# One decoder step on one core: rotary step, softmax scaling, norm squares and residual sums taken from GpSimd, scores of the sample grouped, last squares through TensorE

## The chip, the cores and the metric

One Trainium2 chip, one core of it. The metric is the device time of one execution in microseconds (us), as the median of several runs. TensorE is called PE here, VectorE DVE, ScalarE ACT, GpSimd POOL; SP is the queue from which most transfers are issued.

## The reference, cut to what matters

One layer of a decoder over 264 tokens (256 of a prompt, 8 of a sample, one each), width 2048, all in float32:

```
h = rms_norm(x, g1);  z = h @ w_in          # q (8 heads x 128), k/v of three branches (2 KV heads), gates, u
q, k = partial_rope(first 32 of 128 dims)
o  = sum over 3 branches of gate * softmax(q k / sqrt(128)) v   # compressed blocks, selected blocks, window
d  = pooled mixer of u
m  = concat(o, d) @ w_o
x  = x + rms_norm(m, g2)
a  = relu(rms_norm(x, g3) @ w_up) ** 2      # 2048 -> 8192
y  = x + rms_norm(a @ w_down, g4)           # 8192 -> 2048
```

With 256 prompt tokens all selected blocks are chosen, so the selected branch is plain causal attention. The sample's 8 tokens attend to 256 cached rows each, of both branches, read through a page table. The new cache rows and the window state are outputs too.

## The kernel before, in words

**Linear layers.** Activations lie transposed, features on the 128 partitions and the 264 tokens in the free dimension. Each float32 weight chunk (1 MB, 512 x 512) arrives in a `raw` tile and is converted half by half: ACT writes the rounded high part `wh` (line 195), DVE the rest `wl` (line 193). `linear()` (line 213 on) forms four output tiles in four PSUM banks (`pm`) by three products (high x high, high x low, low x high), each 128 x 264: 24 matmuls per half of a chunk, in four steps of six. All are on line 236. I call the 24 matmuls of one half "a half". The half's two conversions are issued about two halves ahead (`conv_to`).

**What sets the order.** The order is written out by hand. `run()` goes through the steps of a linear layer; at each it calls `tick()`, which does what `later()` put off (evacuations, squares, gains), and then advances the side streams (generators such as `scores00`, `rope_q00`, `sample`, `norm2`) whose entries in the table `AT` (line 36) are due at that step number. Steps 232 to 263 are the last input projection z_q1, 264 to 327 the pool half of w_o, 328 to 391 its attention half, 392 to 423 the first quarter of w_up. Each engine works through its own list in order.

**Attention.** `rope()` (line 500 to 503) rotates 32 partitions of two heads: a shuffle, two products, a sum; of the four calls for q, two are wholly on DVE, and two leave the second and the fourth operation (lines 501 and 503) to POOL. `scores(g, i)` (g: KV head, i: block of 128 queries; a "unit") puts q k into a `px` bank (line 805, two banks in all), adds the mask on DVE, takes the exponential on ACT (line 791), and multiplies each of three parts (16 compressed keys, the selected keys, the window's keys) by the reciprocal sum times the gate `den` (line 824): two parts on DVE, the window's on POOL. `values()` transposes the parts by PE (line 848), evacuates them as high and low halves (`th`, `tl`) and multiplies by the values (lines 208 to 210); the 16 compressed keys go in plain float32 (line 841). `sample_attn()` transposes the cached keys of each of 8 samples and of two branches (line 943), copies them to `kt_` (two buffers), and multiplies each branch's by the two KV heads' queries (`score()`, line 932): 16 calls of two matmuls.

**Norm between w_o and w_up.** The last quarter of w_o is added into `mT` (DVE), each tile squared on ACT, the squares added to `acc0` on POOL (`accumulate()`, line 1162). The last tile's square and the two before are added on DVE (`last_squares`, lines 1175 to 1177) and both sums go through PE, in three banks of one column (line 1221). `rstd_of()` makes 1/sqrt by ACT and DVE. Three DVE operations put it on a diagonal `dg` (line 1239); PE times a matrix of ones spreads it over the partitions (line 1245, tile `pr2`). For each of 16 feature tiles `h2_x` forms mT * r on DVE (line 1258) and adds it to the residual `xT` on POOL (line 1260; the first two on DVE); `h2_hi` rounds on ACT (line 1263), `h2_lo` takes the rest on DVE (line 1268). `h2_before` calls these two tiles at a time, once per half of the first quarter of w_up. Meanwhile halves of the first w_up chunks are converted into spare tiles `xc`, one low part on POOL (`pool_lows`).

**Second norm.** At steps 424 to 443 the stream `norm2` squares the 16 tiles of `xT` on ACT and adds them on POOL (line 1162); its sums go through PE at line 1198.

**Tail.** The last quarter of w_down is added to `m2` (line 1404) and multiplied by the gain (line 1407); the last squares go as above, through three banks (line 1425). Of the eight output pieces of 128 x 512, six are y + o * r on DVE (line 1458), two are a product on ACT and a sum on POOL (line 1452); the sample's outputs (`ts`, `tt`) are made on POOL and transposed by PE (line 1438).

## Time and profile before

| what | value |
|---|---|
| median of 3 runs | 1178.67 us (1178.59 to 1181.34) |
| the profiled execution | 1180.37 us |
| its span in the trace | 1178.6 us |
| mean granted clock of PE | 0.992 |
| PE busy | 1150.8 us, 98% |
| share of PE line 236 in the chain of waits | 71% |
| DVE, ACT, POOL busy | 58%, 46%, 11% |

The profile gives each engine's busy time, the waits of each engine with the instruction that released it, the chain of work that ended last, and for any stretch the busy times with the clock that PE was granted. A share over the whole span says little here: PE has work for nearly all of it, so time can only go where PE waits, where it runs at the lower clock, or where an instruction on PE is dearer than it has to be. These places are few and lie between 205 and 452 us and at the end.

### The profile page before, as it was taken

To read this page: it belongs to the slowest core of one execution; us is meant where nothing else is said; L and a number is where in the kernel's file an instruction comes from. 1 tells how busy PE (TensorE), PEld (TensorE's weight loads), DVE (VectorE), ACT (ScalarE), POOL (GpSimd) and SP (SyncE) were. 2 spreads that over 40 slices of the span, in tenths; PEclk is the share of its full clock that TensorE was granted. 3 is DMA by queue.
4 is the path that set the end of the run, shared out by engine and by line. 5 is a ranking of instruction groups with operands and counts; after the bars stand their busy time and mean duration, and the time that the engine had idled before them with its cause. 6 is when DMAs were issued, how large, how long until landed. Compare 5 with 4: busy or idle time off the path is not lost.

```text
span 1178.6 us, 22160 instructions
## 1 busy us (share of the span) xinstructions
PE 1150.8 (98%) x9303; PEld 1119.4 (95%) x9303; DVE 689.2 (58%) x970; ACT 544.9 (46%) x794; POOL 127.9 (11%) x130
## 2 busy tenths in 40 slices
PE   9999999999999999999999999999999999999996
PEld 8899999887879899999999999999999999999995
DVE  6767667874655776555445554545555445555555
ACT  6545434444446665443335543334453334444442
POOL 0121124220012464000000000000000000000211
PEclk9999999999999999999999999999999999999998
DMA  8866545445545458555555555555555555555542
GB/s 296 236 218 200 169 136 171 129 155 197 163 148 166 139 179 279 202 179 179 179 179 179 179 181 180 181 184 182 184 179 184 184 184 182 170 192 179 178 145 74
DMA packets 115789, 212.09 MB, mean 180 GB/s; under 512 B 7307, under 2 KB 23475, under 8 KB 115553
## 3 DMA queue, kind: packets, MB, share of 16 engines
q1 hardware_dynamic: 114297, 204.68, 53.4%
q0 software_dynamic: 672, 5.27, 1.3%
q8 instruction: 73, 1.20, 0.4%
q10 hardware_dynamic: 720, 0.72, 0.2%
q14 instruction: 27, 0.22, 0.1%
HBM read 206.77 MB, written 8.52 MB: 183 GB/s over the span
## 4 chain that ended last, share of the span: by engine, by line
PE 76%; DVE 3%; POOL 1%; ACT 1%; issue 1%; DVEq 0%; POOLq 0%; ACTq 0%
PE pm L236 71%; PE px L805 1%; PE pa L932 1%; PE px L943 1%; PE px L848 1%; POOL acc L1162 1%; PE pa L1002 1%; DVE orow L1458 0%; POOL xT L1260 0%; PE pa L841 0%; PE px L1333 0%; DVE h2a L1268 0%; DVE eS L824 0%; PE pa L210 0%; PE pa L209 0%
## 5 line engine op out<-in xcount | busy, mean ns | idle before, releaser
L193 DVE TENSOR_TENSOR wl<-raw,wh 128x1024 fp32r<-128x1024 f32 (+1 forms) x355 | 434.5, 1225 | 359.6 <-ACT wh L195 358.6
L195 ACT ACTIVATE wh<-raw 128x1024 fp32r<-128x1024 f32 (+1 forms) x354 | 369.2, 1048 | 463.6 <-PE pm L236 413.9
L236 PE MATMUL pm<-ah,wh 128*128 128x264 f32 x1024 | 292.0, 285 | 0.0
L236 PE MATMUL pm<-al,wh 128*128 128x264 f32 x1024 | 291.1, 284 | 0.0
L236 PE MATMUL pm<-ah,wl 128*128 128x264 f32 x1024 | 291.0, 284 | 0.0
L236 PE MATMUL pm<-h2h,wh 128*128 128x264 f32 x992 | 283.6, 286 | 0.0
L236 PE MATMUL pm<-h2h,wl 128*128 128x264 f32 x992 | 282.5, 285 | 0.0
L236 PEld LDWEIGHTS pm<-ah,wh 128*128 128x128 f32 x1024 | 193.1, 189 | 0.0
L236 PEld LDWEIGHTS pm<-al,wh 128*128 128x128 f32 x1024 | 192.8, 188 | 0.0
L236 PEld LDWEIGHTS pm<-ah,wl 128*128 128x128 f32 x1024 | 192.3, 188 | 0.0
L236 PEld LDWEIGHTS pm<-h2h,wh 128*128 128x128 f32 x992 | 187.7, 189 | 0.4 <-ACT h2h L1263 0.4
L236 PEld LDWEIGHTS pm<-h2h,wl 128*128 128x128 f32 x992 | 186.9, 188 | 0.0
L236 PE MATMUL pm<-h2b,wh 128*128 128x264 f32 x496 | 141.1, 285 | 0.5 <-DVE h2b L1268 0.5
L236 PE MATMUL pm<-h2a,wh 128*128 128x264 f32 x496 | 141.0, 285 | 0.0
L236 PE MATMUL pm<-h_hi,wh 128*128 128x264 f32 x448 | 133.0, 297 | 1.7 <-ACT wh L195 0.7
L236 PE MATMUL pm<-h_hi,wl 128*128 128x264 f32 x448 | 127.7, 285 | 1.3 <-DVE wl L193 1.2
L236 PE MATMUL pm<-h_lo,wh 128*128 128x264 f32 x448 | 127.4, 286 | 0.5 <-DVE h_lo L385 0.5
L1162 POOL TENSOR_TENSOR acc<-acc,sq 128x264 f32<-128x264 f32 x42 | 38.8, 925 | 745.2 <-ACT sq L1158 742.9
L236 PEld LDWEIGHTS pm<-h2b,wh 128*128 128x128 f32 x496 | 93.4, 188 | 0.7 <-DVE h2b L1268 0.7
L236 PEld LDWEIGHTS pm<-h2a,wh 128*128 128x128 f32 x496 | 93.6, 189 | 0.1
L236 PEld LDWEIGHTS pm<-h_hi,wh 128*128 128x128 f32 x448 | 84.8, 189 | 4.3 <-ACT wh L195 1.3
L236 PEld LDWEIGHTS pm<-h_hi,wl 128*128 128x128 f32 x448 | 84.3, 188 | 1.9 <-DVE wl L193 1.9
(573 smaller groups left out, 1396.7 us busy)
## 6 DMA issues: line engine op xcount, KB each, us to landing
raw<-in_w_up SPq DMA_DIRECT2D x64, 1024.0 KB, 5.3
raw<-in_w_down SPq DMA_DIRECT2D x64, 1024.0 KB, 5.1
raw<-in_w_in SPq DMA_DIRECT2D x25, 1024.0 KB, 5.3
raw<-in_w_o SPq DMA_DIRECT2D x16, 1024.0 KB, 5.2
rows<-in_cache_kv SPq DMA_DIRECT2D x64, 128.0 KB, 4.5
out<-in_state_win_kv POOLq DMA_DIRECT2D x8, 510.0 KB, 10.6
raw<-in_w_in SPq DMA_DIRECT2D x5, 512.0 KB, 7.7
rows<-in_state_win_kv SPq DMA_DIRECT2D x8, 256.0 KB, 5.3
```

What stands on the lines that cost most here:

```text
L193: eng.tensor_tensor(wl[:, a_:b_], r[:, a_:b_], wh[:, a_:b_].bitcast(F32), op=ALU.subtract)
L195: nc.scalar.activation(wh[:, a_:b_], r[:, a_:b_], AF.Copy)
L236: nc.tensor.matmul(ps[m_][:, :T], w[:, k, m_ * 128:(m_ + 1) * 128], x[:, k0 + 2 * h + k, :], start=ci == 0 and h == 0 and k == 0 and p == ...
L805: nc.tensor.matmul(pv[:, h, :], zq[g][:, h0 + h, qs], kmat, start=True, stop=True)
L848: nc.tensor.transpose(pp[:kw, h * 128:(h + 1) * 128], e[:, h, :], ident)
L932: nc.tensor.matmul(pS[p0:p0 + 32, 0:256], qm[:, g, 32 * b:32 * b + 32], kt_[:, g * 256:(g + 1) * 256], start=b == 0, stop=b == NB - 1)
L943: nc.tensor.transpose(pp[:, o:o + 128], r[:, 2 * br + c, g * 128:(g + 1) * 128], ident)
L1002: nc.tensor.matmul(po[32 * a:32 * a + 32, :128], ptm[:, a, 32 * b:32 * b + 32], r[:, 2 * (b % 2) + br, g * 128:(g + 1) * 128], start=b == ...
L1162: nc.gpsimd.tensor_tensor(a, a, sq, op=ALU.add)
```

## The change

- **Rotary of q:** all four calls wholly on DVE; the second call of each group is due some steps later (236 and 270); the temporary uses the tag `pT`, now with three buffers.
- **Scaling by `den`:** for the selected and the window part ACT does it, head by head (8 activations per unit); DVE scales the 16 compressed keys only and makes of them `ec`, 48 columns (high, low, high). `vcP` becomes 48 rows (high, high, low), so that the compressed keys take one matmul of the fast float32 kind.
- **Sample's scores:** both branches of one sample together, 8 groups of four matmuls instead of 16 of two; `kt_` has three buffers; `ptm` is cleared later, in the room of `qm`.
- **Norm after w_o:** adds on DVE; the last two squares are not added but go through PE as parts of their own, into three columns of one bank; both held low parts are made at other places; `h2_x` works on two tiles at a time (264 x 2), both operations on DVE; `h2_before` runs in another order; four idle matmuls are dropped.
- **Second norm:** the sum of squares on DVE.
- **Tail:** sums in one bank, one chain for the ten reciprocal roots; the gain of tile 14 on ACT; all eight pieces and `ts`, `tt` on DVE; transfers of the pieces alternate between SP and ACT.
- The entries of `AT` for attention move accordingly.

The diff, cut to its core:

```diff
-            eng = nc.gpsimd if j == 2 else nc.vector
-            eng.tensor_tensor(e, e, den[:, 4 * j:4 * j + 4, None].to_broadcast([128, 4, e.shape[2]]), op=ALU.mult)
+            if j:
+                for h in range(4):
+                    c = 4 * j + h
+                    nc.scalar.activation(e[:, h, :], e[:, h, :], AF.Copy, scale=den[:, c:c + 1])
+            else:
+                nc.vector.tensor_tensor(e, e, den[:, 0:4, None].to_broadcast([128, 4, 16]), op=ALU.mult)
+            if j == 0:
+                ec = ap1.tile([128, 4, 48], F32R, name="ec", tag="ec")
+                st.update(ec=ec)
+                nc.vector.tensor_copy(ec[:, :, 0:16], e)
+                nc.vector.tensor_tensor(ec[:, :, 16:32], e, ec[:, :, 0:16].bitcast(F32), op=ALU.subtract)
+                nc.vector.tensor_copy(ec[:, :, 32:48], ec[:, :, 0:16].bitcast(F32))
...
-        parts = [(eS[:, :, 0:16], 16, [vcP[:, g, :]])]
+        parts = [(st["ec"].bitcast(F32), 48, [vcP[:, g, :]])]
...
-        def score(b, br, kt_):
-            for g in range(2):
-                p0 = 32 * (2 * br + g)
-                nc.tensor.matmul(pS[p0:p0 + 32, 0:256], qm[:, g, 32 * b:32 * b + 32], kt_[:, g * 256:(g + 1) * 256],
-                                 start=b == 0, stop=b == NB - 1)
+        def score(b, kts):
+            for br, kt_ in enumerate(kts):
+                for g in range(2):
+                    p0 = 32 * (2 * br + g)
+                    nc.tensor.matmul(pS[p0:p0 + 32, 0:256], qm[:, g, 32 * b:32 * b + 32],
+                                     kt_[:, g * 256:(g + 1) * 256], start=b == 0, stop=b == NB - 1)
...
-        for k, eng in enumerate((nc.vector, nc.gpsimd)):
-            start(f"rope_q{g}{k}", rope_part(zq[g][:32, 2 * k:2 * k + 2, :], swap, eng))
+        for k in range(2):
+            start(f"rope_q{g}{k}", rope_part(zq[g][:32, 2 * k:2 * k + 2, :], swap, nc.vector))
...
     def accumulate(a, sq):
-        nc.gpsimd.tensor_tensor(a, a, sq, op=ALU.add)
+        nc.vector.tensor_tensor(a, a, sq, op=ALU.add)
...
-    def h2_x(s):
-        t_ = tq.tile([128, T], F32, name="t_", tag="t_")
-        nc.vector.tensor_tensor(t_, mT[:, s, :], rB2[s > 2], op=ALU.mult)
-        eng = nc.vector if s < 2 else nc.gpsimd
-        eng.tensor_tensor(xT[:, s, :], xT[:, s, :], t_, op=ALU.add)
+    def h2_x(k, n=2, mid=None):
+        r_ = pr2[:, :T] if k < 2 else rB2
+        t_ = tq.tile([128, 2, T], F32, name="t2", tag="t2", bufs=1)[:, :n]
+        nc.vector.tensor_tensor(t_, mT[:, k:k + n, :], r_[:, None, :].to_broadcast([128, n, T]), op=ALU.mult)
+        if mid:
+            mid()
+        nc.vector.tensor_tensor(xT[:, k:k + n, :], xT[:, k:k + n, :], t_, op=ALU.add)
...
-    parts = [acc2, last_squares(m2[:, KT - 1, :], sqs)]
+    parts = [acc2, *sqs, sq15]
...
-        nc.gpsimd.tensor_tensor(o, o, y, op=ALU.add)
+            nc.vector.scalar_tensor_tensor(o, o if a < D - 512 else last_o[i], rr[:, i:i + 1], y,
+                                           op0=ALU.mult, op1=ALU.add)
+            (nc.scalar if i else nc.sync).dma_start(y_p[0, i * 128:(i + 1) * 128, a:b], o)
```

Three places where the order of an engine's instructions moves. First DVE at the start of attention, from the rotary of q (tile `zq_188`) to the first masked scores; lines 499 to 503 are `rope()`, 806 and 811 the mask's addition, 192 and 193 a low half. Before:

```order
L500 STREAM_SHUFFLE sw<-zq_188 32x528
L501 TENSOR_TENSOR sw<-sw,cs 32x528
L502 TENSOR_TENSOR zq_188<-zq_188,cs 32x528
L503 TENSOR_TENSOR zq_188<-zq_188,sw 32x528
L500 STREAM_SHUFFLE sw<-zq_188 32x528
L502 TENSOR_TENSOR zq_188<-zq_188,cs 32x528
L193 TENSOR_TENSOR wl<-raw,wh 128x1024 x2
L806 TENSOR_TENSOR eS<-px,cs 128x272
```

and now:

```order
L499 STREAM_SHUFFLE sw<-zq_188 32x528
L500 TENSOR_TENSOR sw<-sw,cs 32x528
L501 TENSOR_TENSOR zq_188<-zq_188,cs 32x528
L502 TENSOR_TENSOR zq_188<-zq_188,sw 32x528
L192 TENSOR_TENSOR wl<-raw,wh 128x1024
L499 STREAM_SHUFFLE sw<-zq_188 32x528
L500 TENSOR_TENSOR sw<-sw,cs 32x528
L501 TENSOR_TENSOR zq_188<-zq_188,cs 32x528
L502 TENSOR_TENSOR zq_188<-zq_188,sw 32x528
L192 TENSOR_TENSOR wl<-raw,wh 128x1024
L811 TENSOR_TENSOR eS<-px,cs 128x2x144 x2
```

DVE's second rotary is whole and comes behind a low half; the pair of heads that is rotated last has changed too (heads 2 and 3 first, then 0 and 1).

Second PE in the sample's scores (line 943, then 961: the four transposes of one sample's keys of a branch; line 932, then 949: the scores; `kt__...`: the copied keys; the other rows are the compressed branch's transposes and product). Before:

```order
L943 MATMUL px<-cs,rows 128x128 x4
L932 MATMUL pa<-kt__3285,qm 32x256 x2
L943 MATMUL px<-cs,rows 128x128 x4
L932 MATMUL pa<-kt__3320,qm 32x256 x2
L956 MATMUL px<-cs,ec_3233 128x64 x2
L943 MATMUL px<-cs,rows 128x128 x4
L932 MATMUL pa<-kt__3329,qm 32x256 x2
```

and now:

```order
L961 MATMUL px<-cs,rows 128x128 x8
L949 MATMUL pa<-kt__3294,qm 32x256 x2
L949 MATMUL pa<-kt__3325,qm 32x256 x2
L961 MATMUL px<-cs,rows 128x128 x4
L975 MATMUL px<-cs,ec_3254 128x64 x2
L961 MATMUL px<-cs,rows 128x128 x4
L949 MATMUL pa<-kt__3336,qm 32x256 x2
L949 MATMUL pa<-kt__3347,qm 32x256 x2
```

Two scores of two column groups stand behind each other, so that four groups follow on four; they wait for the second copy of their own sample, and the two `px` banks are filled back to back more often.

Third DVE in the norm, from the last square to the second tile pair (line 1258, then 1269: mT * r; 1260, then 1272: the residual; 1268, then 1280: the low part; 450 to 456: the reciprocal root; 1239, then 1251: the diagonal). Before, from the last square's sum on:

```order
L1177 TENSOR_TENSOR sq<-sq 128x264
L193 TENSOR_TENSOR wl<-raw,wh 128x512
L451 TENSOR_SCALAR rv<-pm 128x1 x3
L453 RECIPROCAL r<-rv 128x3
L454 SCALAR_TENSOR_TENSOR rv<-r 128x3
L455 TENSOR_TENSOR rv<-rv 128x3
L456 SCALAR_TENSOR_TENSOR r<-rv,r 128x3
L1239 TENSOR_SCALAR t__4733<-cs,r 128x128 x2
L1239 TENSOR_SCALAR t__4733<-cs,r 128x8
L193 TENSOR_TENSOR wl<-raw,wh 128x512
L1258 TENSOR_TENSOR t__4763<-mT,pa 128x264
L1260 TENSOR_TENSOR xT<-xT,t__4763 128x264
```

and now, from the diagonal on:

```order
L1251 TENSOR_SCALAR t__4777<-cs,r 128x128 x2
L1251 TENSOR_SCALAR t__4777<-cs,r 128x8
L192 TENSOR_TENSOR xc_4733<-raw,xc_4733 128x512
L1269 TENSOR_TENSOR t_4795<-mT,pa 128x264
L1272 TENSOR_TENSOR xT<-xT,t_4795 128x264
L1269 TENSOR_TENSOR t_4802<-mT,pa 128x264
L1272 TENSOR_TENSOR xT<-xT,t_4802 128x264
L1280 SCALAR_TENSOR_TENSOR h2a<-xT,gains,h2h 128x264
L1269 TENSOR_TENSOR t_4817<-mT,rB_4786 128x528
L1280 SCALAR_TENSOR_TENSOR h2a<-xT,gains,h2h 128x264
L1272 TENSOR_TENSOR xT<-xT,t_4817 128x528
```

The three sums before the reciprocal root are one now, and from the third tile on the residual's sum stands on DVE, two tiles wide, with the low part of a tile before it in between.

## Rows read from the trace of the kernel before

**Rows 1.** The page's first section: busy us, share of the span and instructions of each engine.

```profile
PE 1150.8 (98%) x9303; PEld 1119.4 (95%) x9303; DVE 689.2 (58%) x970; ACT 544.9 (46%) x794; POOL 127.9 (11%) x130
```

**Rows 2.** The waits of PE, by the line that waits and the instruction that released it: us in total, number of waits, the longest.

```profile
PE px L805 <- POOL zq L503: 2.7, 1, 2.7
PE pa L1198 <- POOL acc L1162: 2.2, 1, 2.2
PE pm L236 <- DVE zq L490: 1.9, 1, 1.9
PE pa L1245 <- DVE t__4733 L1239: 1.8, 1, 1.8
...
PE pm L236 <- DVE h2b L1268: 1.5, 3, 0.5
PE pa L1425 <- DVE sq L1177: 1.5, 1, 1.5
```

**Rows 3.** Stretches of the trace: its length, then the busy time (and instructions) of PE, of PE's weight loads, of DVE, ACT and POOL, then the clock that PE was granted (1.00 is 2.4 GHz), the DMA engines' share and GB/s.

```profile
206.00:391.00 185.00, 180.38 (x1410) 158.24 (x1409) 117.49 (x200) 90.56 (x183) 28.38 (x24) 0.98 0.49 162
217.40:220.77 3.37, 0.92 (x7) 0.92 (x8) 1.74 (x3) 0.00 (x0) 2.32 (x2) 0.99 0.96 308
220.77:224.18 3.41, 3.41 (x16) 3.18 (x15) 2.41 (x7) 1.78 (x9) 0.00 (x0) 0.51 0.69 267
224.18:227.60 3.42, 3.42 (x28) 3.34 (x27) 2.00 (x8) 2.59 (x11) 0.00 (x1) 1.00 0.02 5
244.66:248.07 3.41, 1.53 (x13) 1.20 (x11) 3.41 (x4) 0.59 (x1) 2.51 (x3) 0.99 0.58 225
248.07:251.48 3.41, 3.41 (x15) 3.12 (x14) 3.13 (x6) 0.95 (x1) 2.11 (x2) 0.51 0.02 5
446.04:449.46 3.42, 2.01 (x17) 1.80 (x15) 1.32 (x1) 1.37 (x2) 3.12 (x3) 1.00 0.17 63
449.46:452.87 3.41, 2.60 (x22) 2.61 (x22) 1.30 (x9) 1.21 (x2) 3.40 (x7) 1.00 0.87 264
```

**Rows 4.** The instructions at the start of attention, of DVE, PE and POOL: start and length in us, engine, line, operation, output and inputs; in brackets the idle time before and what ended it.

```profile
209.76 0.76 DVE L500 STREAM_SHUFFLE sw<-zq 32x528 f32<-32x528 f32 x1
212.64 0.75 DVE L500 STREAM_SHUFFLE sw<-zq 32x528 f32<-32x528 f32 x1
214.05 2.34 DVE L193 TENSOR_TENSOR wl<-raw,wh 128x1024 fp32r<-128x1024 f32 x2
215.26 0.62 PE L805 MATMUL px<-kx,zq 128*128 128x272 f32 x2
217.64 2.16 POOL L503 TENSOR_TENSOR zq<-zq,sw 32x528 f32<-32x528 f32 x1
```

**Rows 5.** DVE and ACT around the scaling of a unit, the same columns.

```profile
243.19 0.23 DVE L819 RECIPROCAL den<-den 128x12 f32<-128x12 f32 x1
243.66 3.07 DVE L824 TENSOR_TENSOR eS<-eS,den 128x64 f32<-128x64 f32 x2
...
223.06 0.39 ACT L791 ACTIVATE eS<-eS,nmx 128x128 f32<-128x128 f32 x1
233.61 0.49 ACT L791 ACTIVATE eS<-eS,nmx 128x256 f32<-128x256 f32 x1
```

**Rows 6.** Pieces of the chain of waits in attention: start and length in us, engine, output and line, number of records (a float32 matmul has two).

```profile
237.36 1.05 PE pa L841 x2
...
268.67 0.56 PE pa L932 x4
...
317.65 0.57 PE pa L1002 x16
```

**Rows 7.** Two of PE's matmuls of the fast float32 kind with 512 columns, one behind the other (columns as in rows 4).

```profile
275.69 0.40 PE L208 MATMUL pa<-th,vparts 128*128 128x512 f32 x1
275.93 0.40 PE L209 MATMUL pa<-tl,vparts 128*128 128x512 f32 x1
```

**Rows 8.** Instructions of the norm after w_o, of DVE, POOL and PE (columns as in rows 4).

```profile
397.43 2.71 DVE L1239 TENSOR_SCALAR t__4733<-cs,r 128x128 f32<-128x128 f32 x3
397.55 2.37 POOL L193 TENSOR_TENSOR xc<-raw,xc 128x1024 fp32r<-128x1024 f32 x1 [4.31 <-ACT xc L195]
...
401.16 0.43 DVE L1260 TENSOR_TENSOR xT<-xT,t__4763 128x264 f32<-128x264 f32 x1
...
420.80 0.39 PE L236 MATMUL pm<-h2b,xc 128*128 128x264 f32 x1 [0.48 <-DVE h2b L1268]
424.49 0.39 PE L236 MATMUL pm<-h2b,wh 128*128 128x264 f32 x1 [0.48 <-DVE h2b L1268]
```

**Rows 9.** The adds of the second norm on POOL (columns as in rows 4).

```profile
436.83 13.38 POOL L1162 TENSOR_TENSOR acc<-acc,sq 128x264 f32<-128x264 f32 x12
```

**Rows 10.** The tail on DVE (columns as in rows 4).

```profile
1165.42 0.43 DVE L1176 TENSOR_TENSOR sq<-m 128x264 f32<-128x264 f32 x1
...
1168.48 5.23 DVE L1458 SCALAR_TENSOR_TENSOR orow<-orow,rr,yrow 128x512 f32<-128x512 f32 x4
...
1173.63 1.40 DVE L1458 SCALAR_TENSOR_TENSOR orow<-pm,rr,yrow 128x512 f32<-128x512 f32 x2
```

More of the change, by code (lines that the diff above doesn't have):

```diff
@@ L967, in sample_attn @@
         score(*pend)
+        ptm = ap.tile([128, 4, 288], F32, name="ptm", tag="qm", bufs=1)
+        nc.gpsimd.memset(ptm, 0.0)
         pN = pmisc()
@@ L1215, in nsa_pool_step, with sums @@
     fill = k_rows(lambda r: stg[:, r, :] if r < 4 else tq.tile([128, 512], F32, name="so", tag="so", bufs=2))
-    cols = [pmain()[:, 0:1] for _ in range(3)]
-    last_sq = last_squares(mT[:, KT - 1, :], sqs)
-    def sums(p, first):
-        for o, a in zip(cols, (0, 128, T - 128)):
-            nc.tensor.matmul(o, p[:, a:a + 128], ones[:, 0:1], start=first, stop=not first)
-    low, = held
-    up0 = 2 * ups[0][0][0][0]
-    pool_lows.update(up0 + i for i in (2,))
-    next(fill)
-    sums(acc0, True)
-    flush()
-    mix_gain(KT - 1)
-    next(fill)
-    low(b_=512)
-    sums(last_sq, False)
+    ss = pmain()
+    def sums(p, first, last):
+        for i, a in enumerate((0, 128, T - 128)):
+            nc.tensor.matmul(ss[:, i:i + 1], p[:, a:a + 128], ones[:, 0:1], start=first and i == 0, stop=last,
+                             skip_group_check=True)
+    sq15 = tq.tile([128, T], F32, name="sq", tag="sq", bufs=4)
+    nc.vector.tensor_tensor(sq15, mT[:, KT - 1, :], mT[:, KT - 1, :], op=ALU.mult)
+    flush()
+    for i, p in enumerate((acc0, *sqs, sq15)):
+        sums(p, i == 0, i == len(sqs) + 1)
+    sqs.clear()
+    conv_to(more["from"], held)
+    low0, low2 = held
+    low0()
     r = tq.tile([128, 3], F32, name="r", tag="r3")
-    rstd_of(r, cols)
-    conv_to(more["from"])
+    rstd_of(r, ss[:, 0:3])
+    for _ in range(3):
+        next(fill)
     dg = tq.tile([128, T], F32, name="t_", tag="t_")
@@ L1245, in nsa_pool_step @@
         nc.tensor.matmul(pr2[:, s], ones, dg[:, s], start=True, stop=True)
-    low(a_=512)
-    rB2 = [pr2[:, :T], const.tile([128, T], F32, name="rB2", tag="rB")]
+    low2(b_=512)
+    rB2 = const.tile([128, T], F32, name="rB2", tag="rB")
     class Halved:
@@ L1298, in h2_before @@
             return
[L1299 to L1307 removed]
+        k = 2 * j + 4
+        if k < KT:
+            h2_hi(k)
+            h2_hi(k + 1)
+            if k + 2 < KT:
+                h2_x(k + 2, mid=lambda: h2_lo(k))
+            else:
+                h2_lo(k)
+            h2_lo(k + 1)
     def second_norm():
@@ L1411, in f @@
                         later(1, lambda: add_square(acc2, m2[:, j, :], j, sqs))
-                    later(2 if j < KT - 2 else 4, gain)
+                        later(2, gain)
             return f
@@ L1439, in nsa_pool_step @@
-    os_ = tq.tile([128, 128], F32, name="os_", tag="so", bufs=2)
-    pieces = [(i, a, b) for a, b in ((0, 512), (512, 1024), (1024, 1536), (1536, 2048)) for i in range(2)]
-    pooled = [4, 5]
-    def piece(p):
-        i, a, b = pieces[p]
-        o, y = (rows[n][:, i, a:b] for n in "oy")
-        src = o if a < D - 512 else last_o[i][:, a - D + 512:b - D + 512]
-        return o, src, y, rr[:, i:i + 1], y_p[0, i * 128:(i + 1) * 128, a:b]
-    for p in pooled:
-        o, src, y, r, _ = piece(p)
-        nc.scalar.activation(o, src, AF.Copy, scale=r)
-        nc.gpsimd.tensor_tensor(o, o, y, op=ALU.add)
```

127 lines of the change are left out of this document (59 added, 68 removed).

## The prediction

> **What bounds the kernel now.** I read the busy times first [rows 1]: PE is busy for 98% of the span, DVE for 58%, ACT for 46%, POOL for 11%. The reader should see that no other engine is a bound over the whole, and that what POOL has is small. So time can only be gained where PE waits, where it runs at its lower clock, or where its own instructions get cheaper. Next come the waits of PE [rows 2]: six entries, 2.7 + 2.2 + 1.9 + 1.8 + 1.5 + 1.5 = 11.6 us, and two of them end on POOL itself. Then the windows [rows 3], for the clock: behind the idle time at 217.40 and the one at 244.66 stands a stretch at 0.51, which is the level of 1.2 GHz; behind the idle time at 446.04 (1.41 us of 3.42) stands one at 1.00 (2.4 GHz). A stretch of 3.41 us at 0.51 holds 16 of PE's instructions, the one at 1.00 holds 28, at 3.42 / 28 = 0.122 us: such a fall costs 12 x 0.122 = 1.5 us. Last I read single instructions [rows 4 to 10] for the prices.
>
> **The change, part by part** (gains against the profiled execution of 1180.37 us; a bound from both sides for each).
>
> *Entry of attention.* Before, DVE starts the first rotary at 209.76 and the second at 212.64 [rows 4], so a whole one takes 2.88 us. POOL's last operation ends at 217.64 + 2.16 = 219.80, and PE, which has begun the scores at 215.26, waits 2.7 us for it [rows 2]. Now DVE does both with a low half between them: 2.34 / 2 = 1.17 us each in a pair [rows 4]. The second ends at 209.76 + 2.88 + 1.2 + 2.88 = 216.7. The scores of its heads come first and still stand where 215.26 was: a wait of about 1.5. Behind two score banks PE must wait for DVE to empty one: the first evacuation can start only at about 217, some 0.6 more. So 2.7 becomes 2.1. Then the wait for z_q1's evacuation, 1.9: DVE has the scaling of the unit, 3.07 us for two operations beside POOL [rows 5], before it. That turns into a product and three casts of 64 columns, 0.2 each by the nearest row (0.23 [rows 5]); with what remains of `den` ahead PE waits about 0.9 and once more 0.65, so 0.3 is gained. The new idle times are in two pieces each with PE's work between; I put them nearer to the 1.41 us that no fall followed than to the whole 2.45 and 1.88 of the other two [rows 3], and count both falls as gone: 0.6 + 0.3 + 1.5 + 1.5 = **3.9**, with bounds 0.9 (both falls stay) and 7.6 (no wait left at all).
>
> *Compressed values.* One float32 matmul per unit takes 1.05 us in two records [rows 6]. Now it is one of the fast kind with 512 columns, which start 0.24 us apart [rows 7]. 48 rows instead of 16 cost nothing visible there, as 128 rows run at that pace. Four units: 4 x 0.81 = **3.2**; bounds 2.5 (at the lower clock) and 3.2.
>
> *Sample's scores.* 16 groups of 0.56 us [rows 6] become 8 groups of four matmuls in four column groups. The nearest row has 16 records of 128 columns in four column groups, which take 0.57 [rows 6]; here 8 records of 256. So 16 x 0.56 - 8 x 0.57 = 4.4. But a group now waits for the second copy of its own sample, with both `px` banks in use; I take 0.4 for half of the groups, the time of one transposing piece, 1.5 in all: **2.9**, bounds 0 and 4.4.
>
> *Norm after w_o.* The three products for the diagonal take 2.71 us on DVE, while POOL makes a low half for 2.37 of it [rows 8]. Small operations elsewhere take about 0.2 (0.23 [rows 5]), so without POOL they take 0.6: 2.1 gained. The sums are ready about 0.6 earlier, as two adds and a product on DVE (0.43 each [rows 10]) become one product, but three more matmuls and a low part of 0.3 to 0.4 come ahead of the first tile: the first w_up matmul starts about 2.25 earlier. From there the halves come 424.49 - 420.80 = 3.69 us apart [rows 8], and PE waits 0.48 in each: DVE sets the pace there. Now DVE has per half two operations of 528 columns, two low parts of about 0.43 and one low half of 1.17 [rows 4, 8]. For 528 columns I take 0.62: 528 of 1024 columns at 1.17 are 0.60, and joining two operations of 0.43 saves one start. That is 2 x 0.62 + 2 x 0.43 + 1.17 = 3.27 per half, and five such halves gain 5 x 0.42 = 2.1. The Trainium skill (Perfetto Trace Analysis, section "Optimizing Scalar/DVE Operations") puts the overhead of one DVE operation on SBUF at about 60 ns; by that figure the joined operation would take 0.86 - 0.06 = 0.80, a half 3.63, five halves would gain 0.3, and the whole sum would be 15.7 and the time 1163.0, an estimate. The rows speak for more than that page: between 264 columns at 0.43 and 1024 at 1.17 a start comes to 0.17, and no run here has shown a joined pair. Sum **4.3**; bounds 2 (the pace stays) and 5.5 (PE's own 2.9 is reached).
>
> *Second norm.* POOL's adds, 13.38 / 12 = 1.1 us each [rows 9], end at 450.2, and PE waits 2.2 for them [rows 2]. On DVE an add takes 0.43 [rows 8]; 16 of these and five low halves of 1.17 are 6.9 + 5.9 us in some 15: it keeps up. **2.2**; bounds 0 and 2.4.
>
> *Tail.* Two adds of 0.43 [rows 10] are not on the way any more, and one root chain instead of three saves a little, the three further matmuls cost as much: 0.8. The eight pieces took 1168.48 to 1175.03, 6.55 us; four of them at 5.23 / 4 = 1.31, the last two at 0.70 without POOL [rows 10]. Now eight at 0.70 with `ts` and `tt` at 0.2: 6.0 less a little that overlaps. Transfers alternate between two queues, so the last two go out side by side. **1.5**; bounds 0 and 2.5.
>
> *The rest.* The last unit (1,1) is crowded into fewer steps, and its scales fall on ACT while the sample's sums run: **-0.5**, bounds -2 and 0. The adds of w_o's squares on DVE (13 x 0.43 = 5.6 us) lie under PE's work of the last quarters: DVE is busy for 117 of 185 us from 206 to 391 [rows 3].
>
> Sum: 3.9 + 3.2 + 2.9 + 4.3 + 2.2 + 1.5 - 0.5 = 17.5; 1180.37 - 17.5 = 1162.9. The median of the runs lies 1.7 below the profiled execution, so the forecast is **1161.2**.
>
> **The rivals.**
>
> *A: ACT's queue.* ACT takes its work in order. Eight scales per unit cost 8 x 0.39 = 3.1 us for one block of keys and 8 x 0.49 = 3.9 for two [rows 5]; what stands behind them, the high halves for PE, the exponentials of the next unit, the evacuated transposes of `values`, comes later by this. If a unit of each kind is on the way, 7.0 are lost: 1168.2. For: two `px` banks only, and the product on DVE took 3.07 for two parts. Against: ACT has 90.6 busy us of 185 [rows 3], and high halves are made two halves ahead.
>
> *B: DVE falls behind.* The change gives DVE what POOL did in one stretch, 206 to 391, where 40 halves run (8 of z_q1, 32 of w_o). If every half's low part came late by t, PE would lose 40 t; slower than before by over 0.3% needs 17.5 + 3.5 = 21 us, t = 0.53. At t = 0.6 the loss is 24 and the time 1185.2. For: in the crowded places DVE is the one that PE waits for (z_q1's evacuation, the low parts of h2 [rows 2]). Against: it is busy for 64% of that stretch, and POOL had 28.4 us there, which take DVE less than half of that by 0.43 against 1.1. The Trainium skill (Perfetto Trace Analysis, section "Optimizing Scalar/DVE Operations") says the opposite of what this change does: if DVE is saturated, giving work to Scalar or even GPSIMD may make sense. The trace does not show it saturated over that stretch, only in pieces of some 3 us (3.41 of 3.41 at 244.66 [rows 3]).
>
> *C: more.* All waits and falls at the entry go (7.6 in place of 3.9), the sample's groups wait for nothing (4.4 in place of 2.9): 5.2 more, 1156.0.
>
> *D: nothing in attention.* Between 206 and 330 something else sets the pace (conversions, the copies of keys, the transfers of weights), and the first three gains, 3.9 + 3.2 + 2.9 = 10.0, come back as waits: 1171.2. For: DMA at 0.96 at 217.40. Against: PE is busy for 180.4 of 185 us [rows 3].
>
> *E: it does not do what it says.* The moved parts only replace a wait on POOL by as long a one on DVE: within 3.5 us of 1178.67.
>
> **How the numbers follow.** A run of this kernel tells 0.3%, 3.5 us, from no change. Chances: my sum 0.57, A 0.18, C 0.13, D 0.05, E 0.04, B 0.03. The likeliest case's own range is 1158 to 1166. The range reaches down to C with its lower side (1154.5) and up past A to 1170; D, E and B and a little of the tails are left out. Faster by over 0.3%: 0.57 + 0.18 + 0.13 + 0.05 = 0.93; the same 0.04; slower 0.03.
>
> **What would show it.** Right: no wait of PE on POOL is left; the wait at the first scores is about 1.5 and the stretches behind it and behind z_q1 are at 1.00; the compressed product is a single record at 0.24; 8 score groups of 0.57; the three products of the diagonal take 0.6 and the first halves of w_up stand 3.3 apart; the eight pieces take 0.7 each. Wrong: a wait of PE on ACT's scales or on `th` of several us (A), low halves named over and over among PE's releasers between 206 and 391 (B), the freed time of attention back as waits on key copies (D).

## The result

The changed kernel takes 1161.88 us (median of 6 runs, 1160.77 to 1163.47); the kernel before took 1180.57 us beside it. The ratio is 0.9844, with a 95% interval of 0.983 to 0.9857: 1.6% faster, 18.7 us. Forecast were 1161.2 us and a range of 1154.5 to 1170.0.

### The profile page after: what moved, and what is told of

It reads as the page before. It is cut to its first block, busy times and chain, and to the rows that moved or that the text cites. A ratio compares the mean times of both kernels' runs of the same rounds, so it can differ in the third digit from the quotient of the medians.

```text
span 1160.0 us, 22100 instructions
## 1 busy us (share of the span) xinstructions
PE 1140.8 (98%) x9303; PEld 1116.5 (96%) x9303; DVE 691.5 (60%) x1023; ACT 552.6 (48%) x822; POOL 50.2 (4%) x61
## 3 DMA queue, kind: packets, MB, share of 16 engines
q10 hardware_dynamic: 1008, 1.25, 0.3%
HBM read 206.77 MB, written 8.52 MB: 186 GB/s over the span
## 4 chain that ended last, share of the span: by engine, by line
PE 90%; DVE 4%; DMA 2%; issue 1%; ACT 1%; POOL 0%; SPq 0%; DVEq 0%; ACTq 0%; POOLq 0%
PE pm L235 82%; DVE wl L192 1%; DMA raw<-in_w_in 1%; PE pa L208 1%; PE pa L207 1%; PE pa L209 1%; PE px L961 1%; PE px L810 1%; ACT wh L194 1%; PE px L864 1%; DMA sp<-in_state_pool 1%; PE px L577 1%; PE pa L949 0%; DVE orow L1457 0%; PE pa L1023 0%
## 5 line engine op out<-in xcount | busy, mean ns | idle before, releaser
L235 PEld LDWEIGHTS pm<-h_lo,wh 128*128 128x128 f32 x448 | 84.2, 188 | 1.0 <-DVE h_lo L384 0.7
```

The lines of the kernel that those rows point to most:

```text
L235: nc.tensor.matmul(ps[m_][:, :T], w[:, k, m_ * 128:(m_ + 1) * 128], x[:, k0 + 2 * h + k, :], start=ci == 0 and h == 0 and k == 0 and p == ...
```

## The profile after

The profiled execution took 1161.75 us, its span is 1160.0, that is 18.6 us less than before. The page's first section, against [rows 1]:

```profile
PE 1140.8 (98%) x9303; PEld 1116.5 (96%) x9303; DVE 691.5 (60%) x1023; ACT 552.6 (48%) x822; POOL 50.2 (4%) x61
```

POOL has lost 78 us of busy time; on balance DVE has gained 2 and ACT 8, as some of DVE's own instructions became shorter or went to ACT. The waits of PE, columns as in [rows 2]:

```profile
PE px L1466 <- DVE tt L1464: 2.5, 1, 2.5
PE pm L235 <- DVE wl L192: 1.4, 3, 0.8
PE px L645 <- DVE hx L641: 1.4, 1, 1.4
PE px L810 <- DVE zq L502: 1.2, 1, 1.2
...
PE pa L1444 <- DVE acc L1181: 0.6, 1, 0.6
PE px L961 <- DVE kt__3347 L964: 0.5, 1, 0.5
```

No wait on POOL is left. Of those of [rows 2] two stand here still, but shorter: the wait for the rotary (line 502), 1.2 instead of 2.7, and the one of the tail's sums (line 1444), 0.6 instead of 1.5. The one at line 645 is new. The first, in the tail, delays nothing but the sample's transpose. The stretches at the places of [rows 3], and around the norm (same columns):

```profile
217.40:220.77 3.37, 2.77 (x18) 2.48 (x19) 3.27 (x8) 0.41 (x2) 0.00 (x0) 1.00 0.62 241
220.77:224.18 3.41, 3.41 (x29) 3.33 (x28) 3.19 (x7) 2.33 (x9) 0.00 (x0) 1.00 0.10 10
244.66:248.07 3.41, 3.41 (x26) 3.02 (x25) 2.42 (x4) 2.86 (x5) 0.00 (x0) 1.00 0.00 0
248.07:251.48 3.41, 3.41 (x28) 3.24 (x27) 3.34 (x7) 1.06 (x1) 0.00 (x0) 1.00 0.00 0
382.15:385.56 3.41, 3.16 (x29) 2.87 (x29) 2.66 (x10) 2.77 (x6) 0.32 (x1) 1.00 0.18 35
385.56:388.97 3.41, 3.41 (x19) 3.35 (x17) 2.66 (x8) 1.59 (x4) 0.00 (x0) 0.50 0.93 297
```

Both falls of the clock at the entry of attention are gone; PE works through at 1.00. Ahead of the tail one fall is left, from 385.6 on, in the norm behind w_o.

Where the time went is best read from the same matmul in both traces. Both kernels have 8256 matmuls of the linear layers, in the same order (line 236, now 235); the table has the start of the n-th (counted from 0), and what each stretch between two of them gained. It is worked out from the starts in the two traces.

| n | what begins there | before | after | gained since the row above | forecast |
|---|---|---|---|---|---|
| 1200 | before the first scores | 212.34 | 213.49 | -1.15 | 0 |
| 1344 | first w_o matmul, z_q1 is done | 243.20 | 241.68 | 2.67 | entry, together 3.9 |
| 1368 | w_o, one half on | 250.51 | 245.63 | 3.37 | |
| 2088 | last half of w_o | 390.18 | 378.68 | 6.62 | 3.2 + 2.9 - 0.5 = 5.6 |
| 2112 | first w_up matmul | 402.20 | 389.62 | 1.08 | norm, together 4.3 |
| 2304 | eight halves on | 430.38 | 414.55 | 3.25 | |
| 2600 | behind the second norm | 472.19 | 453.91 | 2.45 | 2.2 |
| 8255 | last matmul | 1164.06 | 1145.88 | -0.10 | 0 |
| end | | 1178.60 | 1159.99 | 0.43 | 1.5 |

Summed over PE's records from 205 us to the end of w_o (each counted up to the start of the next), the compressed products went from 4.20 to 1.71 us, the sample's score groups from 8.57 to 5.34 and the transposes between them from 8.57 to 7.63: 2.5 + 3.2 + 0.9 = 6.6 in all. One of the four compressed products, 0.6 of it, lies ahead of the first w_o matmul and so belongs to the entry in the table; the other 6.0 are most of the 6.62 of the stretch up to the last half of w_o.

## The experiments

Each is the changed kernel with one edit, unless it says otherwise; `...` in a diff marks what is left out. The starts of the first few hundred matmuls differ by up to 3.2 us between the profiles, so what a single edit does is read between two matmuls of its stage, as in the table above, and the ratio to the kernel before stands beside it.

**The rotary back on POOL (rope_pool).**

```diff
-        for k in range(2):
-            start(f"rope_q{g}{k}", rope_part(zq[g][:32, 2 * k:2 * k + 2, :], swap, nc.vector))
+        for k, eng in enumerate((nc.vector, nc.gpsimd)):
+            start(f"rope_q{g}{k}", rope_part(zq[g][:32, 2 * k:2 * k + 2, :], swap, eng))
...
```

Left out are two entries of `AT`: the second call of each group is due at 232 and 266 again, as before.

> The changed kernel with the second rotary of each group of q given back to POOL (and the two entries of the table that belong to it). Theory (the entry of attention gained twice: a shorter wait and the clock fall behind it): the wait of PE for POOL's rotary is 2.7 us again in place of 1.2, the stretch behind it falls to 0.51, and the stage loses 1.5 + 1.5 = 3.0 us; 1165 us. Rival (the clock fall had another cause, such as the transfer at 0.96 of the DMA share): the wait is 2.7 us, the stretch stays at 1.00, and only 1.5 us are lost; 1163.4 us.

Measured: 1165.03 us, ratio 0.9869 (0.9853 to 0.9886). The wait, and the stretches of the trace there:

```profile
PE px L810 <- POOL zq L502: 3.0, 1, 3.0
```

```profile
217.40:220.80 3.40, 0.50 (x4) 0.51 (x5) 0.69 (x2) 0.00 (x0) 2.76 (x2) 0.99 0.89 289
220.80:224.20 3.40, 3.40 (x16) 3.17 (x15) 2.63 (x8) 1.69 (x5) 0.00 (x0) 0.50 0.05 20
```

The entry loses 2.86 us, the second group's rotary another 1.08. With the wait of 3.0 the fall comes back. The theory holds: the gain was a shorter wait and, with it, no fall. The load of the transfers, the rival's cause, is not ruled out by this run alone, since the stretch with the wait has the DMA engines at 0.89 (0.96 before [rows 3]); but the falls of scale_pool and acc_pool2 below follow stretches at 0.41 and 0.25, so transfers near their limit are not needed for one.

**The scaling back on DVE and POOL (scale_pool).**

```diff
-            if j:
-                for h in range(4):
-                    c = 4 * j + h
-                    nc.scalar.activation(e[:, h, :], e[:, h, :], AF.Copy, scale=den[:, c:c + 1])
-            else:
-                nc.vector.tensor_tensor(e, e, den[:, 0:4, None].to_broadcast([128, 4, 16]), op=ALU.mult)
+            eng = nc.gpsimd if j == 2 else nc.vector
+            eng.tensor_tensor(e, e, den[:, 4 * j:4 * j + 4, None].to_broadcast([128, 4, e.shape[2]]), op=ALU.mult)
```

> The changed kernel with the scaling of the selected part on DVE and of the window part on POOL again; the rest, the three casts too, stays. Theory (the scaling of unit (0,0) on DVE beside POOL held up the evacuation of z_q1): PE waits about 1.9 us for it again or a little more, as the casts stand there too, the next stretch falls to 0.51, and 3.4 us are lost there; 1165.3 us or slower. Rival (ACT's eight scales per unit cost PE as much elsewhere, and the order in the table made the gain): no wait there, and time within 1 us of the changed kernel or faster.

Measured: 1171.05 us, ratio 0.9916 (0.9899 to 0.9932). A row of DVE's list and two of POOL's, at the scaling of one unit:

```profile
243.87 2.34 DVE L834 CAST ec<-eS 128x64 fp32r<-128x64 f32 x1
```

```profile
243.74 1.90 POOL L829 TENSOR_TENSOR eW<-eW,den 128x1024 f32<-128x1024 f32 x1 [13.98 <-DVE den L825]
245.57 0.58 POOL L1136 MEMSET qm<- 128x576 f32 x1
```

```profile
245.10:248.50 3.40, 1.25 (x10) 1.03 (x11) 3.37 (x6) 0.59 (x1) 1.05 (x2) 0.99 0.41 160
248.50:251.90 3.40, 3.40 (x17) 3.40 (x17) 3.37 (x7) 0.60 (x1) 0.00 (x0) 0.51 0.02 5
```

A cast of 64 columns that otherwise takes 0.2 takes 2.34 here: it ends at 246.21, 0.57 behind POOL's product and 0.06 behind the clearing that POOL does next. The stretch of the last two rows loses 4.16 us, with its fall; the first unit loses 1.25 more, the last two 1.09 and 2.79: 9.4 in all, nearly three times what I expected, as each unit's first cast now stands behind POOL (1.02, 2.34, 0.94 and 2.31 us in the four). The Trainium skill (SBUF — State Buffer, "Who interferes with whom") says that DVE and GpSimd share a pair of ports as an exclusive lock, that a cast can take it, and that the other engine then fully blocks; the rows agree, here with POOL first, 0.13 us ahead of the cast. ACT, in contrast, needs 1.71 and 1.69 us for the two parts of a unit in the changed kernel, and no wait of PE on them stands among its waits: rival A fell.

```profile
241.36 1.71 ACT L831 ACTIVATE eS<-eS,den 128x256 f32<-128x256 f32 x4 [1.86 <-DVE den L825]
242.97 1.69 ACT L831 ACTIVATE eW<-eW,den 128x256 f32<-128x256 f32 x4
```

**The sample's scores by branch (score16).**

```diff
-            for br, kt_ in enumerate(kts):
-                for g in range(2):
-                    p0 = 32 * (2 * br + g)
-                    nc.tensor.matmul(...)
+            for g in range(2):
+                p0 = 32 * (2 * br + g)
+                nc.tensor.matmul(...)
...
+                if pend:
                     score(*pend)
+                pend = (b, br, kt_)
```

> The changed kernel with the sample's scores by branch again: 16 groups of two matmuls in two column groups; three buffers for the copied keys and all else stay. Theory (the score matmuls cost 0.54 us a group with the switch behind them, 16 against 8 at 0.67): these go back from 5.3 to 8.6 us on PE, the transposes between them lose another 0.9, and 4 us are lost; 1166 us. Rival (the groups only moved waits on the copies): under 2 us, with fewer waits on copied keys in its place.

Measured: 1166.74 us, ratio 0.9883 (0.9867 to 0.99). Between the 1464th and the 1560th matmul 3.77 us are lost. Later, at the sample's value rows, this profile is 0.73 shorter than the changed kernel's, but that isn't owed to the edit: rope_pool (0.79) and acc_pool2 (0.74) are, too. The theory holds.

**The copy earlier (hx3_early).**

```diff
         nc.vector.tensor_tensor(hx, hx, hu, op=ALU.mult)
+        if slot:
+            hx3 = tp.tile([128, 2, 3, 16], F32, name="hx3", tag="hx3", bufs=1)
+            nc.vector.tensor_copy(hx3, ...)
         yield
...
-            hx3 = tp.tile([128, 2, 3, 16], F32, name="hx3", tag="hx3", bufs=1)
-            nc.vector.tensor_copy(hx3, ...)
```

> The changed kernel with the copy that makes three times 16 columns of the compressed values' hidden layer issued one step earlier, right behind the product that it copies. Theory (this copy stood on DVE behind two low halves and a copy, and PE waited 1.4 us for it at 163 us, a wait that the kernel before did not have): the wait is gone, 1.3 us gained by then; 1160.6 us. Rival (PE would wait for DVE in any case there, for a low half next): the wait moves to another line, under 0.5 us gained.

Measured: 1160.27 us, ratio 0.9831 (0.9814 to 0.9847). The new wait of the changed kernel, on PE and on DVE:

```profile
164.81 0.61 PE L645 MATMUL px<-w2t,hx 128*48 128x128 f32 x4 [1.37 <-DVE hx L641]
```

```profile
163.00 1.22 DVE L192 TENSOR_TENSOR wl<-raw,wh 128x1024 fp32r<-128x1024 f32 x1
164.13 0.41 DVE L637 COPY vcR<-px 128x256 f32<-128x256 f32 x1
164.47 0.20 DVE L641 COPY hx<-hx 128x96 f32<-128x96 f32 x1
```

and the same matmul with the copy issued earlier, without a wait:

```profile
164.06 0.64 PE L646 MATMUL px<-w2t,hx 128*48 128x128 f32 x4
```

1.41 us are gained there. Its span is 2.4 us shorter than the changed kernel's in all; the rest is 0.78 at the sample's value rows and some 0.9 at the norm, where this run has no fall, less 0.7 at the start. The two medians are 1.6 us apart and their intervals overlap; what is shown is the 1.41 us.

**The residual tile by tile (h2_single).**

```diff
-        nc.vector.tensor_tensor(t_, mT[:, k:k + n, :], r_[:, None, :].to_broadcast([128, n, T]), op=ALU.mult)
+        for i in range(n):
+            nc.vector.tensor_tensor(t_[:, i], mT[:, k + i, :], r_, op=ALU.mult)
...
-        nc.vector.tensor_tensor(xT[:, k:k + n, :], xT[:, k:k + n, :], t_, op=ALU.add)
+        for i in range(n):
+            nc.vector.tensor_tensor(xT[:, k + i, :], xT[:, k + i, :], t_[:, i], op=ALU.add)
```

> The changed kernel with the residual's operations after w_o tile by tile, all still on DVE: two operations of 264 columns wherever one of 528 stood. Theory (the halves came 3.7 us apart because POOL's adds slowed DVE, and joining pairs is worth only a start, 0.08 us by the pace of rows): the halves of the first quarter of w_up stand 3.18 + 2 x 0.08 = 3.35 us apart, 0.16 more for some five halves, 0.8 us lost; 1162.7 us. Rival (the prediction's reading, joining saves 0.24 for each of two operations): 3.66 us apart, 2.4 us lost; 1164.3 us.

Measured: 1164.28 us, ratio 0.9869 (0.9851 to 0.9886). The low parts of the weights on DVE, one per half, in the changed kernel:

```profile
401.22 1.21 DVE L192 TENSOR_TENSOR xc<-raw,xc 128x1024 fp32r<-128x1024 f32 x1
404.40 1.22 DVE L192 TENSOR_TENSOR xc<-raw,xc 128x1024 fp32r<-128x1024 f32 x1
```

and tile by tile:

```profile
403.02 1.23 DVE L192 TENSOR_TENSOR xc<-raw,xc 128x1024 fp32r<-128x1024 f32 x1
406.34 1.23 DVE L192 TENSOR_TENSOR xc<-raw,xc 128x1024 fp32r<-128x1024 f32 x1
```

3.18 us apart against 3.32: joining a pair is worth 0.07 for each operation, near the 60 ns that the Trainium skill states (Perfetto Trace Analysis, "Optimizing Scalar/DVE Operations"), and not the 0.24 of my reading of the rows. The stage loses 1.3 us in all, against 0.8 by the theory and 2.4 by the rival. The median is the rival's number, but not by its cause: the profile of this run lost 1.24 us in the first 400 matmuls, far ahead of the edit. By the pace of the halves the theory holds and the rival fell.

**The residual's sum on POOL (h2_pool).**

```diff
-        nc.vector.tensor_tensor(xT[:, k:k + n, :], xT[:, k:k + n, :], t_, op=ALU.add)
+        (nc.vector if k < 2 else nc.gpsimd).tensor_tensor(xT[:, k:k + n, :], xT[:, k:k + n, :], t_, op=ALU.add)
```

> The changed kernel with the sum of the residual, two tiles wide, on POOL again from the third tile on; DVE keeps the products and low parts. Theory (POOL beside DVE stretches DVE's low parts and low halves): low parts of two take 1.4 us instead of 0.9, low halves 1.5 instead of 1.2, the halves of the first quarter stand 3.6 us or more apart, and 2 to 4 us are lost; 1164 to 1166 us. Rival (DVE had the pace by its own number of operations): with 0.62 less on DVE per half it keeps up with PE, the halves stand 2.95 apart, and 1 us is gained.

Measured: 1170.45 us, ratio 0.9918 (0.9901 to 0.9934). DVE's low parts beside POOL, and then two of the changed kernel's, without POOL:

```profile
397.71 1.96 DVE L1280 SCALAR_TENSOR_TENSOR h2a<-xT,gains,h2h 128x264 fp32r<-128x264 f32 x2
401.35 1.96 DVE L1280 SCALAR_TENSOR_TENSOR h2b<-xT,gains,h2h 128x264 fp32r<-128x264 f32 x2
```

```profile
408.72 0.89 DVE L1280 SCALAR_TENSOR_TENSOR h2b<-xT,gains,h2h 128x264 fp32r<-128x264 f32 x2
```

DVE has one operation less and yet its halves stand 3.64 us apart, since two low parts take 1.96 instead of 0.89. With the rows of the experiment before (3.32 with twice the operations and no POOL), this settles that term: the halves came 3.69 apart before [rows 8] because POOL worked beside DVE, and hardly because there were two operations where one would do. From the first w_up matmul to eight halves on 3.97 are lost, as expected; this run has no fall at the norm, which gives 1.58 back. The loss of the whole is larger for another reason. POOL's list goes on, behind its last sum, with the transfers of the window state:

```profile
410.23 3.90 POOL L1356 DMA_DIRECT2D out<-in_state_win_kv  x8
```

and ACT then waits for a weight load, 8.52 us:

```profile
430.98 1.06 ACT L194 ACTIVATE wh<-raw 128x1024 fp32r<-128x1024 f32 x1 [8.52 <-DMA raw<-in_w_up]
```

That load took 17.2 us from issue to landing by the chain of waits; loads of w_up take 5.2 in the median in the changed kernel. PE loses 2.95 and 3.29 us in the two halves there, a fall from 431 on included.

**The second norm's sum on POOL (acc_pool2).**

```diff
-            accumulate(acc1, square(xT[:, k, :]))
+            s_ = square(xT[:, k, :])
+            nc.gpsimd.tensor_tensor(acc1, acc1, s_, op=ALU.add)
```

> The changed kernel with the second norm's 16 adds on POOL again; all else stays. Theory (POOL's adds at 1.1 us each were late by the wait that PE had): PE waits 2.2 us for the last add again and 2.4 us are lost; 1164.3 us. Rival (the adds were slow only because other work of the norm on POOL came before them, which is gone): POOL begins earlier, ends in time, and under 0.5 us is lost.

Measured: 1166.93 us, ratio 0.9888 (0.9872 to 0.9905). The wait is back, and here a fall follows it (before, none did [rows 3]):

```profile
PE pa L1209 <- POOL acc L1325: 2.2, 1, 2.2
```

```profile
432.40:435.80 3.40, 1.22 (x11) 1.01 (x9) 1.31 (x1) 0.14 (x1) 3.24 (x5) 0.99 0.25 46
435.80:439.20 3.40, 3.40 (x17) 3.40 (x17) 2.27 (x9) 1.21 (x2) 3.40 (x7) 0.51 1.10 407
```

4.0 us are lost there, 2.2 + 1.5 and a little. The adds are late on their own; that other work on POOL came before them was not the cause.

**The rows' piece later (fill_later).**

```diff
-    next(fill)
     h2_x(0, 1)
     h2_hi(0)
+    next(fill)
```

> The changed kernel with the fourth piece of the key rows (four transposes and their copy on ACT) issued behind the first residual tile and its rounding, no longer ahead of them. Theory (the first w_up matmul came 1.1 us earlier instead of 2.2 because this copy of 0.6 stood on ACT ahead of the rounding, and four transposes on PE): the first matmul starts 0.4 to 0.6 us earlier, and the gain stays in part; 1161.4 us. Rival (the granted clock of 0.5 at that place is what holds it): nothing is gained, the start moves by under 0.2.

Measured: 1163.34 us, ratio 0.9861 (0.9844 to 0.9877). The first w_up matmul comes 7.36 us behind the last of w_o, against 8.14 in the changed kernel; but this run has no fall, and the runs of other kernels without one have 6.56 there with nothing changed in the norm (score16, hx3_early). So the piece stood in nobody's way: moved, it puts the first matmul 0.8 later, and all but 0.1 of that comes back in the halves behind. My theory fell: what held the first matmul up in the changed kernel goes with the fall, 8.14 - 6.56 = 1.58 us. In the five experiments that have the fall this distance is 7.75 to 8.20.

**Compressed values in plain float32 (cmp16).**

```diff
-        parts = [(st["ec"].bitcast(F32), 48, [vcP[:, g, :]])]
+        parts = [(eS[:, :, 0:16], 16, [vcP[:, g, :]])]
...
```

Left out are the threefold copy and the three casts, which go, and the 16 rows of `vcP`, which come back.

> The changed kernel with the compressed values in plain float32 with 16 rows again (no threefold columns, no three casts of 64 columns); scaling on ACT and all else stay. Theory (the new form saves 4.20 - 1.71 = 2.5 us of PE's time in four units, and costs 1.4 us of a new wait at 163 us): by 168 us 1.4 gained, then 2.5 lost, 1.1 in all; 1163 us. Rival (the three casts on DVE or the evacuation on ACT stood in somebody's way): less is lost or something gained behind 230 us; the time is 1161 us or lower.

Measured: 1166.96 us, ratio 0.9874 (0.9852 to 0.9896). Between the 400th and the 900th matmul 1.4 us are gained, as expected, and each of the four units loses 0.61 to 0.63 at its product, 2.5 for the four. But between the 1632nd and the 1680th matmul 6.39 us are lost:

```profile
291.79 3.89 POOL L1347 DMA_DIRECT2D out<-in_state_win_kv  x8
```

```profile
PE pa L1014 <- DMA rows<-in_cache_kv: 3.6, 1, 3.6
```

In the changed kernel a clearing of `acc` on POOL, which waits for the last product of the sample, stands ahead of the window state's transfers until 325.2:

```profile
325.20 0.32 POOL L1172 MEMSET acc<- 128x264 f32 x1 [34.15 <-PE pa L1023]
```

Without the tiles that this edit leaves out, the clearing does not wait (both clearings of `acc` run from 291.3 on); the transfers go out at 291.8, PE waits 3.6 us for the sample's value rows, and a fall follows at 314.5. Neither theory nor rival had that.

**Fewer parts in the sums, and the other rotary first (sum2_swap).**

```diff
-'rope_q00': [236], 'rope_q01': [230]
+'rope_q00': [230], 'rope_q01': [236]
...
+    nc.vector.tensor_tensor(sq15, sq15, sqs[0], op=ALU.add)
-    parts = [acc2, *sqs, sq15]
+    parts = [acc2, sq15]
```

> The changed kernel with two edits that lie far apart and are read by stage. First, the square of tile 14 is added to that of tile 15 on DVE, in both norms with a last square, so that two parts instead of three go through PE's sums; theory (three columns of one more part cost PE 0.7 us, one add on DVE 0.35): the first w_up matmul and the tail's reciprocal root come about 0.3 us earlier each; rival (the part of tile 14 ran under DVE's work): no gain or 0.1 lost. Second, heads 0 and 1 are rotated first and heads 2 and 3 behind a low half; theory (the first scores wait 1.2 for the rotary that comes second, although they could start on the other pair): the wait falls to about 0.6 and the entry gains 0.6; rival (the next score banks wait for DVE in any case): under 0.2. Together 1160.7 us.

Measured: 1162.82 us, ratio 0.9836 (0.9813 to 0.9859). Neither edit gives anything: the tail gains 0.05 us, the first w_up matmul loses 0.05, and the entry gains 0.04. The wait for the rotary falls from 1.2 to 0.7, but that for DVE's emptying of a score bank grows from 0.3 to 0.7. Both rivals hold.

**The window state's transfers held back (shift_late).**

```diff
+        hold = tq.tile([128, 8], F32, name="hold", tag="hold", bufs=1)
+        nc.gpsimd.tensor_copy(hold, m2[:, KT - 1, 0:8])
         for b in range(NB):
```

> The changed kernel with one small POOL copy ahead of the eight transfers of the window state, which reads the last tile of the first w_down block, so that they can't be issued before it is there. In the changed kernel they go out at 325.7 us, in the one before at 450.2, as POOL's list is empty earlier. Theory (at 325 us these 8 MB of traffic meet the loads of w_o's and the sample's rows, the DMA engines stand at 0.94, and PE's stretch from 315 to 331 us takes 0.8 longer than in the kernels that had POOL busy): 0.8 us gained there and nothing lost later; 1161.1 us. Rival (that stretch is a matter of what ACT and the evacuations do there): no change at 315 to 331.

Measured: 1167.08 us, ratio 0.9881 (0.9858 to 0.9905). At the sample's value rows 0.25 us are gained, not 0.8. That stretch differs by 0.1 to 0.8 us in profiles whose edits do not touch it, and here, too, PE waits 0.5 in it for these rows. At the new place:

```profile
582.90 3.90 POOL L1358 DMA_DIRECT2D out<-in_state_win_kv  x8
```

```profile
604.96:608.37 3.41, 0.55 (x5) 0.34 (x3) 1.66 (x3) 2.06 (x3) 0.00 (x0) 0.96 0.82 311
608.37:611.78 3.41, 3.35 (x16) 3.35 (x17) 3.15 (x7) 2.65 (x7) 0.00 (x0) 0.54 0.51 138
```

The chain of waits goes through one load of weights there:

```profile
587.30 18.22 DMA raw<-in_w_up
...
605.63 1.06 ACT wh L194
```

It lands after 18.2 us, where such loads take 5.2 in the median; PE stands still for 3 us and its clock falls: 4.7 us lost. With h2_pool (410.2) and cmp16 (291.8) three places for these transfers cost 4.7 to 6.4 us each, the falls included. The changed kernel's own, 325.7, costs nothing that I can see, like the one at 450.15 before.

**Two edits together (hx3_idle):** the copy of hx3_early and

```diff
         sums(p, i == 0, i == len(sqs) + 1)
+        if i:
+            idle_pe(1, lambda: pacc('pS'))
```

> The changed kernel with the two edits that the runs so far favour: the threefold copy of the compressed values' hidden layer one step earlier (1.4 us at 163 us), and two idle matmuls of 128 columns among the one-column sums of the norm behind w_o, against the fall to 0.51 that the changed kernel shows from 385.6 on and that five of the twelve other profiles do not show there. Theory (behind 18 records of one column the clock falls at that place although PE is recorded as busy; wide records between them hold it): no fall there, the first w_up matmul 6.6 to 7.0 us behind the last of w_o instead of 8.1; 1159.5 us. Rival (the fall is a matter of where in the program's time the norm lies, as the kernel with the earlier copy has none without any idle matmul): the idle matmuls put 0.2 to 0.4 us on the way and give nothing; 1160.7 us.

(Counted over all profiles, the fall is absent in six of the eleven others, not five of twelve.) Measured: 1160.82 us, ratio 0.9829 (0.9808 to 0.9851), its profile as long as that of hx3_early to 0.1 us. From the last half of w_o to the first w_up matmul it loses 0.45 to hx3_early, which has no fall there without idle matmuls. The rival holds, as to the gain; whether they would have held the clock is not settled, as this run may have had no fall without them.

## Why the prediction was right, point by point

- **Entry of attention** (3.9 forecast, 6.0 measured, 0.6 of it the first unit's compressed product). Both falls went, as I took it. The wait for the rotary is 1.2, and 0.3 for a bank, against the 2.1 that I had, and the second wait is not 1.55 but gone: DVE has no scaling in front of z_q1's evacuation, and the casts are done in time. Rope_pool and scale_pool put the two causes back one by one, with their falls.
- **Compressed values** (3.2, measured 2.5). The step that failed is the pace: a product stands on the way for 1.71 / 4 = 0.43 us; 0.24 is the pace of two such matmuls one behind the other [rows 7], and here no like one follows. And the sum had no term for the threefold copy, which cost 1.4 at 163 us (hx3_early). Net, this part gave 1.1.
- **Sample's scores** (2.9, measured 3.2 + 0.9 from the transposes between). A group takes 5.34 / 8 = 0.67 with what follows it, not 0.57; the waits on copies are 0.5, not 1.5. Score16 loses 3.77 with both.
- **Norm behind w_o** (4.3, measured 4.3, but from other places). The products for the diagonal took 0.62, as forecast. The first w_up matmul came 1.1 earlier, not 2.25, because of the fall from 385.6 on (1.58). The stage then gained 1.3 in the first half, where the kernel before had its own fall, which I had counted at nothing; it stands in the kernel before behind the idle time of the diagonal:

```profile
398.26:401.67 3.41, 1.62 (x14) 1.54 (x15) 3.38 (x6) 0.20 (x2) 1.65 (x1) 0.99 0.00 0
401.67:405.08 3.41, 3.41 (x17) 3.02 (x15) 3.18 (x8) 2.64 (x6) 1.48 (x2) 0.51 0.90 223
```

  The halves stand 3.18 apart (3.27 forecast), but my price of joining was wrong; the gain came from POOL's leaving. That the term fits to 0.1 us is luck.
- **Second norm** (2.2, measured 2.45): right; acc_pool2 loses more, since a fall joins.
- **Tail** (1.5, measured 0.43): the step that failed is that the reciprocal roots would be ready 0.8 earlier. Before, they were ready 4.39 us behind the last matmul's start (1164.06 to 1168.45), now 4.32 (1145.88 to 1150.20). The sums on PE wait for the last add of the squares, now on DVE, and then run as 18 records:

```profile
1146.78 0.38 PE L1444 MATMUL pa<-ones,acc 128*128 128x1 f32 x2 [0.62 <-DVE acc L1181]
...
1148.59 0.37 PE L1446 MATMUL pa<-sq,ones 128*128 128x8 f32 x2
...
1150.23 1.42 DVE L1457 SCALAR_TENSOR_TENSOR orow<-orow,rr,yrow 128x512 f32<-128x512 f32 x2
```

  Those take as long as the adds that they replace (sum2_swap). The pieces took 1150.23 to 1156.14, 5.9 us, as forecast; the last transfers end 3.85 us behind them, not earlier than the 3.57 of before: that two queues let them go side by side gave nothing.
- **The rest** (-0.5): no loss is to be seen in the last unit. **Missed:** POOL's list. The transfers of the window state stand behind POOL's other work, and with that gone they moved from 450 to 325.7 us. I did not price that, and the runs show places where it would have cost 4.7 to 6.4 us. That 325.7 is none of them is luck.
- **Rivals:** A fell (scale_pool, and no wait on ACT's scales); B, too: low halves hold PE up for 1.4 us in the whole program; D and E fell, as attention alone gained 12.7 with no wait on POOL left. C came true in part: at the entry 1.5 us of waits are left, and the sample's groups and the transposes between them gave 4.1 of its 4.4.
- **The sum.** The mechanism holds: waits and falls at the entry, POOL's load on DVE's pace, and cheaper forms on PE are where the time went, and each was put back by a run. How near the number came is in part luck: by the table, entry and attention gave 12.7 instead of 9.5, while the time up to the first scores, with the threefold copy (-1.15), and the tail (0.43 instead of 1.5) took 2.2 of that back. And the 1.7 that I took off, as the runs' median before lay below the profiled execution, came from three runs; the six runs beside the changed kernel have 1180.57, above it.

## What to carry to other kernels

When work leaves an engine that is rarely busy, look at what stands behind it in that engine's list: transfers that it issues go out earlier, and where they land decides as much as the work moved. Price an operation moved to DVE by rows of DVE without the slower engine beside it, since more than half of some rows here was that neighbour (2.71 against 0.62, 1.96 against 0.89). And count a wait of PE together with the clock fall that follows it, but leave room for the fall to come or not.
